# Level products of two heads in one group, in place, with the samples behind the last level and branch b first: a hybrid HGRN2 / RG-LRU layer

## The chip, the cores and the metric

One core of one Trainium2 chip. The metric is the device time of one execution in microseconds; a kernel's time is the median of its runs. The comparison is between the kernel before and the kernel after one change, both computing the same outputs.

## The reference

One layer of a decoder trunk runs on 512 prompt tokens and 8 sample tokens (one new token each for eight running sequences), all in fp32. Width is 1024, with eight heads of 128 and eight blocks of 128.

```python
h = _rmsnorm(x, norm1_g[l]) * (1.0 + sc1) + sh1
u = h @ w_in[l]                                  # 1024 x 8192
qa, fa, ia, oga, xb, yb, ga, gb = _split_cols(u)
# HGRN2: S_t = diag(f_t) S_{t-1} + k_t outer v_t,  o_t = S_t^T q_t
o, S_new = _hgrn2(q, k, v, logf, S0)
o_a = _rmsnorm(o, hg_onorm_g[l]) * silu(oga)
# RG-LRU: causal convolution, block-diagonal gates, then a linear recurrence
hseq, h_last = _rglru(xc, r, ig, lru_lambda[l], st_lru)
o_b = hseq * gelu(yb)
merged = sigmoid(ga) * (o_a @ w_branch_a[l]) + sigmoid(gb) * (o_b @ w_branch_b[l])
x = x + g1 * (merged @ w_out[l])
h2 = _rmsnorm(x, norm2_g[l]) * (1.0 + sc2) + sh2
x = x + g2 * (square(relu(h2 @ w_ff1[l])) @ w_ff2[l])
y = _rmsnorm(x, final_norm_g)
```

sh, sc and g come from a product of the conditioning vectors with w_mod (the modulation). The outputs are y for prompt and samples and the new states: the HGRN2 matrices, the RG-LRU vectors and the convolution's last inputs.

## The kernel before

Everything is kept with channels on the partitions and the 520 tokens (T = 512 + 8) in the free dimension. A big product is one 128 x 128 weight tile against 260 tokens (half of T). fp32 accuracy is had from three products of split operands: `whi` is the rounded weight (cast on ACT, L111), `wlo` the remainder (a subtraction on DVE, L114); activations are split in the same way (`split`, L200 on ACT and L201 on DVE). The helper `gemm` issues these products at L150.

The stages follow one another in one list of steps: the norm and modulation; then for h = 0 to 7 the head's four column blocks (f, q, g, v) and, in between, the blocks of RG-LRU (`rg_x`, `rg_y`); then eight merge gates (`ga`, part 6 of w_in), within which `end_recurrences` and `begin_tail` close the pools of the heads; then branch a (o_a times w_branch_a), the eight gates of part 7, and branch b; then w_out and the MLP. The order on each engine is set by a scheduler that puts work with a higher priority first (`urgent()` is an offset of 200) and otherwise follows the program. Weights are fetched ahead on SP's queue. `mod_step` puts parts of the second modulation's products (L408, on the `wst` buffers) between the steps of the tail.

A head's prompt part (`head_prompt`) works with blocks that double, from b = 1 to b = 64. At each level TensorE computes, for every block of 2b tokens, the attention between its two halves (K of the first half, Q of the second, L642 for b = 2 to 16, L656 for b = 1, L674 for b = 32 and L680 for b = 64). Then DVE multiplies one half of the Q and K rows by a running decay (L682), which writes the buffer Y from X, or X from Y at the next level; the half that isn't multiplied is copied along (L688; at b = 1 by ACT). `copy_predicated` (L690) puts the level's products into `a32` under a mask. After the last level the diagonal blocks go to `at`, K is transposed, the chunk states S are built, the outputs are made (L726 and L728), squared on ACT with a sum (L733), normalized by a small chain on DVE (L734 and L206 to L215, inverse square root) and scaled on ACT (L738), transposed (L742), and multiplied into the output gate (L744), which is stored to `oaT_d` in DRAM (L745).

The sample part of a head: v of the samples is transposed and copied (`vs`, L592), sent to DRAM and broadcast back to all partitions (`vd` L594, `vb` L596, both on SP's queue), and the state tiles `st` are scaled on ACT (L603) and updated on DVE (L604, eight per head); then 8 products (L610) give the outputs, which are copied to `sev`, transposed (L615) and put into `os` (L617).

In the tail, `load_branches` loads o_a and o_b back from DRAM on POOL's queue through five buffers `t` (L878 for o_a), and splits them into the tiles `a` (o_a) and `b` (o_b).

Of the kernel before, what the change touches and what calls it, by code (L numbers as in the profile page):

```python
# [28 lines left out]
URGENT = 200  # L29
NWM = 8  # L30
# [12 lines left out]
BUFS = {"e": 6, "g": 6, "xb": 1, "xc": 2, "xcs": 2, "gate": 4, "ag": 2, "hs": 3, "y": 3, "ma": 8, "rs": 1, "sq": 1, "t": 5, "sqs": 2,  # L43
# [32 lines left out]
class Kernel:  # L76
# [108 lines left out]
    def urgent(self):  # L185

        return self.tc.high_priority(offset=URGENT)

# [354 lines left out]

# [7 lines left out]
    def head(self, h, first=None):  # L551
# [17 lines left out]
        v = self.slot(self.hg, "e")  # L569
# [10 lines left out]
        fkq = self.fkq[h % 2]  # L580
# [3 lines left out]
        self.head_prompt(h, f, X, q, v, og)  # L584
        self.head_sample(h, st, vb, fkq)
# [14 lines left out]
    def head_sample(self, h, st, vb, fkq):  # L600
        nc = self.nc
        for b in range(NB):
            nc.scalar.activation(st[:, b], st[:, b], AF.Copy, scale=fkq[:, 0, b:b + 1])  # L603
            nc.vector.scalar_tensor_tensor(st[:, b], vb[:, b], fkq[:, 1, b:b + 1], st[:, b], OP.mult, OP.add)  # L604
        nc.sync.dma_start(self.o["hgrn_s"][0, :, h].rearrange("b k v -> k b v"), st)

        po = self.pps.tile([128, 512], F32, name="ps")
        for b in range(NB):
            j, c = 32 * (b % 4), 128 * (b // 4)
            nc.tensor.matmul(po[j:j + 32, c:c + 128], fkq[:, 2], st[:, b], start=True, stop=True)  # L610
        ev = self.hg.tile([128, 256], F32, name="sev")
        nc.scalar.copy(ev, po[:, :256])
        pt = self.ppt.tile([128, 512], F32, name="pt")
        for c in (0, 128):
            nc.tensor.transpose(pt[:, c:c + 128], ev[:, c:c + 128], self.ident)  # L615
        own = bass.AP(tensor=pt.tensor, offset=pt.offset, ap=[pt.ap[0], [132, 2], [33, 4]])
        nc.vector.tensor_copy(self.os[:, h].rearrange("p (a b) -> p a b", a=2), own)  # L617

    def head_prompt(self, h, f, X, q, v, og):
        nc = self.nc  # L620

        pv = self.pps.tile([128, 512], F32, name="ps")
        for c in range(NC):
            nc.tensor.transpose(pv[:, c * C:(c + 1) * C], v[:, c * C:(c + 1) * C], self.ident)
        vn = self.slot(self.hg, "g")
        nc.scalar.copy(vn[:, :L], pv)

        Y = self.hg.tile([128, 2, T], F32, name="Y", bufs=2)  # L630
        nc.vector.tensor_tensor(X[:, 0, :L], q[:, :L], f[:, :L], OP.mult)
        T_ = self.hg.tile([128, 508], F32, name="tb", bufs=2)
        tb, to = f[:, :L], 0
        a32 = self.hg.tile([128, NC, 32], F32, name="a32")
        at = self.at[h % 2]

        def block_level(x, y):
            p = self.pps.tile([128, 512], F32, name="ps")
            for c in range(NC):
                for j in range(4):  # L640
                    s = slice(c * C + 32 * j, c * C + 32 * j + 32)
                    nc.tensor.matmul(p[32 * j:32 * j + 32, c * 32:c * 32 + 32], x[:, s], y[:, s], start=True, stop=True)  # L642
            return p[:, :128].rearrange("p (c t) -> p c t", c=NC)
# [6 lines left out]

        p = self.pps.tile([128, 512], F32, name="ps")
        for c in range(NC):
            for j in range(4):
                s = c * C + 32 * j
                o = p[32 * j:32 * j + 32, c * 64:c * 64 + 64].rearrange("p (x t) -> p x t", x=2)
                nc.tensor.matmul(o, X[:, 1, s:s + 32], X[:, 0::2, s:s + 32], start=True, stop=True)  # L656
        first = p[:, :256].rearrange("p (c x t) -> p c x t", c=NC, x=2)
        nc.vector.tensor_tensor(a32, first[:, :, 1], self.mdiag, OP.mult)
        b = 1
        while b < C:  # L660
            Q, K = X[:, 0], X[:, 1]

            n = L // (2 * b)
            fac = bass.AP(tensor=tb.tensor, offset=tb.offset, ap=[tb.ap[0], [1, 2], [2, n], [0, b]])
            if b == 1:
                p = first[:, :, 0]
            elif b <= 16:
                p = block_level(K, Q)
            elif b == 32:
                p = self.pps.tile([128, 512], F32, name="ps")  # L670
                for c in range(NC):
                    for j in (0, 64):
                        s = c * C + j
                        nc.tensor.matmul(p[j:j + 32, c * 32:c * 32 + 32], K[:, s:s + 32], Q[:, s + 32:s + 64],  # L674
                                         start=True, stop=True)
            else:
                p = self.pps.tile([128, 512], F32, name="ps")
                for c in range(NC):
                    s = c * C
                    nc.tensor.matmul(p[:64, c * 64:c * 64 + 64], K[:, s:s + 64], Q[:, s + 64:s + 128],  # L680
                                     start=True, stop=True)
            nc.vector.tensor_tensor(view(Y, b, 0, 2 * b, n, b), view(X, b, 0, 2 * b, n, b), fac, OP.mult)  # L682
            if b == 1:
                nc.scalar.copy(view(Y, 0, 1, 2, n, 1), view(X, 0, 1, 2, n, 1))
            else:

                h2 = b // 2
                nc.vector.tensor_copy(view(Y, h2, b, 2 * b, n, h2), view(X, h2, b, 2 * b, n, h2))  # L688
            if b <= 16:
                nc.vector.copy_predicated(a32, self.masks[b], p)  # L690
            elif b == 32:
                for j in (0, 64):
                    nc.scalar.copy(at[j:j + 32, :, j + 32:j + 64],
                                   p[j:j + 32, :128].rearrange("p (c t) -> p c t", c=NC))
            else:
                nc.scalar.copy(at[:64, :, 64:], p[:64, :256].rearrange("p (c t) -> p c t", c=NC))
            t2 = tb.rearrange("p (n two) -> p n two", two=2)
            tn = T_[:, to:to + n]
            nc.vector.tensor_tensor(tn, t2[:, :, 0], t2[:, :, 1], OP.mult)
            tb, to = tn, to + n  # L700
            X, Y = Y, X
            b *= 2
        Q, K = X[:, 0], X[:, 1]
        for j in range(0, 128, 32):
            nc.vector.tensor_copy(at[j:j + 32, :, j:j + 32], a32[j:j + 32])
# [54 lines left out]
    def blockdiag_w(self, n):  # L760
        nc = self.nc
        r = []
        for name in ("lru_wa", "lru_wx"):
            st = self.hg.tile([128, 128], F32, name="bdst")
            nc.sync.dma_start(st, self.i[name][0, n])
            hi = self.hg.tile([128, 128], F32R, name="bdh" + name)
            lo = self.hg.tile([128, 128], F32R, name="bdl" + name)
# [7 lines left out]
    def blockdiag(self, w, x, bias):  # L775
        nc = self.nc
        o = self.slot(self.hg, "gate")
# [9 lines left out]
    def rg_x(self, n):  # L787
# [4 lines left out]
        xb = self.slot(self.hg, "xb")  # L792
        with self.urgent():
            nc.scalar.copy(self.two(xb), ps)
        xc = self.slot(self.hg, "xc")
# [9 lines left out]
        xs = self.split(xc, self.hg, "xcs")  # L805
# [5 lines left out]
    def rg_scans(self, ns):  # L811
# [3 lines left out]
        for n in ns:  # L815
            r = self.rg[n][0]
            a = self.slot(self.hg, "ag")
            self.grouped(nc.scalar.activation(a, r, AF.Exp, scale=self.c8n[:, n:n + 1]))
            self.grouped(nc.scalar.activation(r, r, AF.Tanh, scale=self.c8[:, n:n + 1]))
            u = self.slot(self.hg, "xc")  # L820
# [8 lines left out]
        for n, (a, u) in zip(ns, aa):  # L829
            g = self.rg[n][1]  # L830
            nc.vector.tensor_tensor(g, g, u, OP.mult)
            hs = self.slot(self.hg, "hs")
# [7 lines left out]
    def rg_y(self, n):  # L840
# [3 lines left out]
        t, y = self.slot(self.hg, "y"), self.slot(self.hg, "y")  # L844
# [29 lines left out]
    def load_branches(self):  # L874
        nc = self.nc
        for h in range(H):
# [3 lines left out]
            self.oa.append(self.split(t, self.ab, "a"))  # L880
        for n in range(KO):
            t = self.slot(self.tail, "t")
            nc.gpsimd.dma_start(t, self.obT_d[n])
            self.ob.append(self.split(t, self.abb, "b"))
# [11 lines left out]
    def merge(self, m, s, t1):  # L896
        self.branch("w_branch_b", m, self.ob, s)
# [652 lines left out]
    def run(self):  # L1550
# [39 lines left out]
        for m in range(KO):  # L1590
            one("w_in", 48 + m, lambda m: ga.update({m: self.gate(6, m, self.slot(self.ma, "ma"))}), m)
# [5 lines left out]
        for m in range(KO):  # L1597
            if m == 2:
                steps.append(([], self.rg_out))
            one("w_branch_a", m, lambda m: self.branch("w_branch_a", m, self.oa, ga[m]), m)  # L1600
            if m <= TAIL or m % 2:
                mod_step()
        for m in range(KO):
            one("w_in", 56 + m, lambda m: gb.update({m: self.gate(7, m, self.slot(self.tail, "t"))}), m)
            one("w_branch_b", m, lambda m: self.merge(m, gb.pop(m), ga.pop(m)), m)
# [24 lines left out]
    def begin(self):  # L1630
# [167 lines left out]
        self.hg = self.open_pool("hg", 2, reuse_waits="tile")  # L1798
        self.at = []
        self.fkq = [self.hg.tile([128, 3, 32], F32, name=f"fkq{n}", bufs=1) for n in range(2)]  # L1800
        for t in self.fkq:
# [70 lines left out]
```

## Time and profile before

| | |
|---|---|
| median of three runs | 1030.33 us (1029.38 to 1030.82) |
| profiled execution, its own time | 1028.26 us |
| its span | 1026.5 us |
| granted TensorE clock, mean | 0.997 |
| PE / DVE / ACT / POOL busy | 1004.4 / 691.1 / 520.4 / 123.3 us |
| heads, 62 to 420 us: PE busy | 356.71 of 358 us |

The profiled execution is one run of the program; its span is the time from its first to its last instruction. Busy times are of that span. L numbers are lines of the kernel; PE is TensorE's matmul, DVE VectorE, ACT ScalarE, POOL GpSimd, SP the queue from which most DMAs are issued. The records of small products come in twos: 16 matmuls of L642 are 32 records.

### The profile page before, as it was taken

How to read it: one execution, taken by the hardware profiler on the slowest of the kernel's cores; microseconds unless marked ns; L12 is line 12 of the kernel's file. 1: busy time of each engine (PE TensorE's matmuls, PEld its weight loads, DVE VectorE, ACT ScalarE, POOL GpSimd, SP SyncE). 2: the span in 40 equal slices, each digit the busy share in tenths (PEclk: the TensorE clock that was granted, in tenths of full speed). 3: DMA queues.
4: the chain of work that ended last, by engine and by line, in shares of the span. 5: the costliest groups of instructions: out<-in, count | busy, mean ns of one | idle time of the engine just before them, and what ended most of it. 6: DMA issues, size and time to landing. Idle time of an engine off the chain costs nothing. (4 is left out here: it accounts for less than half of the span.)

```text
span 1026.5 us, 23725 instructions
## 1 busy us (share of the span) xinstructions
PE 1004.4 (98%) x9756; PEld 967.8 (94%) x9756; DVE 691.1 (67%) x1520; ACT 520.4 (51%) x988; POOL 123.3 (12%) x228
## 2 busy tenths in 40 slices
PE   5999999999999999999999999999999999999997
PEld 3899999999999999988999999999999999999996
DVE  6788779596877868365233347677776776777685
ACT  4555743663575356342122235466556655656663
POOL 3200000000000000031000001011421231232150
PEclk9999999999999999999999999999999999999998
DMA  9673443434334324398555568222672484274242
GB/s 323 223 202 111 120 128 115 118 113 141 107 115 127 115 85 136 97 331 248 164 165 165 165 186 242 86 83 63 134 186 72 94 183 115 53 162 96 63 82 84
DMA packets 201823, 143.68 MB, mean 140 GB/s; under 512 B 6767, under 2 KB 189703, under 8 KB 201707
## 3 DMA queue, kind: packets, MB, share of 16 engines
q1 hardware_dynamic: 191090, 128.08, 41.7%
q0 software_dynamic: 10608, 14.05, 6.9%
q8 instruction: 76, 1.25, 0.5%
q14 instruction: 33, 0.26, 0.1%
q10 hardware_dynamic: 16, 0.03, 0.0%
HBM read 123.61 MB, written 11.26 MB: 131 GB/s over the span
## 5 line engine op out<-in xcount | busy, mean ns | idle before, releaser
L150 PE MATMUL mm<-h,whi 128*128 128x260 f32 (+1 forms) x2944 | 489.9, 285 | 0.0
L150 PEld LDWEIGHTS mm<-h,whi 128*128 128x128 f32 x2944 | 409.4, 188 | 4.8 <-ACT whi L111 3.3
L150 PE MATMUL mm<-h,wlo 128*128 128x260 f32 x1472 | 304.8, 286 | 0.3 <-DVE wlo L114 0.3
L111 ACT CAST whi<-wst 128x1024 fp32r<-128x1024 f32 x164 | 171.7, 1049 | 221.8 <-PE mm L150 172.9
L114 DVE TENSOR_TENSOR wlo<-wst,whi 128x1024 fp32r<-128x1024 f32 x164 | 200.0, 1220 | 108.7 <-ACT whi L111 107.6
L150 PEld LDWEIGHTS mm<-h,wlo 128*128 128x128 f32 x1472 | 230.2, 189 | 2.1 <-issue 0.8
L150 PE MATMUL mm<-a,whi 128*128 128x260 f32 x512 | 84.2, 285 | 0.0
L150 PEld LDWEIGHTS mm<-a,whi 128*128 128x128 f32 x512 | 70.3, 188 | 2.1 <-issue 1.2
L150 PE MATMUL mm<-a,wlo 128*128 128x260 f32 x256 | 51.9, 283 | 0.0
L878 POOL DMA_DIRECT2D t<-oaT_d x8 | 4.4, 552 | 384.1 <-ACT sq L751 376.4
L1271 DVE TENSOR_TENSOR f<-f 128x260 f32<-128x260 f32 x64 | 27.3, 427 | 27.6 <-ACT f L1266 26.9
L1260 ACT ACTIVATE ft<-ft,fsh 128x512 f32<-128x512 f32 (+2 forms) x36 | 24.0, 676 | 36.1 <-DVE ft L1257 36.1
L150 PE MATMUL mm<-b,whi 128*128 128x260 f32 x256 | 41.1, 282 | 0.0
L1263 POOL TENSOR_TENSOR ft<-ft,fsh 128x8 f32<-128x8 f32 x28 | 18.4, 658 | 188.2 <-DVE ft L1257 188.2
L150 PEld LDWEIGHTS mm<-a,wlo 128*128 128x128 f32 x256 | 39.5, 188 | 0.0
L150 PEld LDWEIGHTS mm<-b,whi 128*128 128x128 f32 x256 | 35.0, 188 | 0.0
L1305 POOL DMA_DIRECT2D ma<-snap x28 | 26.7, 968 | 38.3 <-issue 29.1
L1287 POOL DMA_DIRECT2D ma<-snap x28 | 25.9, 925 | 36.0 <-DMA ma<-snap 24.4
L603 ACT ACTIVATE st<-st,fkq 128x128 f32<-128x128 f32 x64 | 20.2, 390 | 16.6 <-DVE fkq L582 14.4
L1266 ACT ACTIVATE f<-ft 128x520 f32<-128x520 f32 (+1 forms) x36 | 20.8, 587 | 15.0 <-POOL ft L1264 13.0
L894 DVE TENSOR_TENSOR t<-mm,t 128x520 f32<-128x520 f32 x8 | 5.6, 700 | 30.5 <-PE mm L150 30.5
L150 PE MATMUL mm<-b,wlo 128*128 128x260 f32 x128 | 25.9, 284 | 0.0
(579 smaller groups left out, 1933.1 us busy)
## 6 DMA issues: line engine op xcount, KB each, us to landing
wst<-in_w_in_dram SPq DMA_DIRECT2D x64, 512.0 KB
wst<-in_w_mod_dram SPq DMA_DIRECT2D x32, 512.0 KB
wst<-in_w_ff_dram SPq DMA_DIRECT2D x64, 256.0 KB
wst<-in_w_ff_dram SPq DMA_DIRECT2D x32, 512.0 KB
wm<-in_w_mod_dram SPq DMA_DIRECT2D x16, 512.0 KB
st<-in_state_hgrn_dram SPq DMA_DIRECT2D x8, 512.0 KB
vb<-vd SPq DMA_DIRECT2D x8, 512.0 KB
out_dram<-st SPq DMA_DIRECT2D x8, 512.0 KB
```

Source lines behind the costliest of these rows:

```text
L111: ins = self.nc.scalar.copy(hi, st)
L114: self.nc.vector.tensor_tensor(lo, st, hi.bitcast(F32), OP.subtract)
L150: self.last_product = self.nc.tensor.matmul(ps[s][:, :c.stop - c.start], x, y[:, c], start=first and n == 0, stop=last and n == 2)
L603: nc.scalar.activation(st[:, b], st[:, b], AF.Copy, scale=fkq[:, 0, b:b + 1])
L878: nc.gpsimd.dma_start(t[:, :L], self.oaT_d[h])
L894: self.nc.vector.tensor_tensor(self.two(s), ps, self.two(s), OP.mult)
L1260: nc.scalar.activation(t[:, :p], t[:, :p], AF.Relu, bias=sh[:, 0:1])
L1263: eng.tensor_tensor(t[:, p:], t[:, p:], sh[:, 1:9], OP.add)
L1266: nc.scalar.activation(f, self.two(self.ft)[:, a:a + n], AF.Square)
L1271: self.nc.vector.tensor_tensor(f[:, n], f[:, a], f[:, b], op)
L1287: nc.gpsimd.dma_start(x[1][:, b], v[:, :n], accum_op=OP.add)
L1305: nc.gpsimd.dma_start(x[t][:, a], s[p], accum_op=OP.add)
```

## The change

In the heads: the prompt part is called once for two heads, (h - 1, h), after the second head's inputs are there. At each level the products of both heads form one group (`together()`, priority offset 400): 32 products for b = 1 to 16, 16 for b = 32, 8 for b = 64, and behind the last the samples' 16 products of both heads (L623). Q and K are multiplied in place: Y, the copies of L688 and the ACT copy at b = 1 are gone, and X has four buffers. `a32` and `at` hold both heads, and one `copy_predicated` serves two heads. f and v move to `ma` buffers, the RG-LRU's tiles to a pool of their own, and the samples' transposes (L632) come after both heads' outputs. The samples' state update (L597) is issued before the levels.

In the tail: the eight gates issued in the heads' pools are now part 7, and branch b comes first; the merge then adds branch a. o_b is loaded into the tiles `a`, o_a into `b`.

```diff
-BUFS = {"e": 6, "g": 6, ...
+BUFS = {"e": 4, "g": 6, ...
+    def together(self):
+        return self.tc.high_priority(offset=TOGETHER)
...
-        f = self.slot(self.hg, "e")
-        X = self.hg.tile([128, 3, T], F32, name="X", bufs=2)
+        f = self.slot(self.ma, "ma")
+        X = self.hg.tile([128, 3, T], F32, name="X", bufs=4)
...
-        self.head_prompt(h, f, X, q, v, og)
-        self.head_sample(h, st, vb, fkq)
+        ... (transposes of v, vn, X[:, 0] = q * f)
+        for b in range(NB):
+            nc.scalar.activation(st[:, b], st[:, b], AF.Copy, scale=fkq[:, 0, b:b + 1])
+            nc.vector.scalar_tensor_tensor(st[:, b], vb[:, b], fkq[:, 1, b:b + 1], st[:, b], OP.mult, OP.add)
+        nc.sync.dma_start(self.o["hgrn_s"][0, :, h].rearrange("b k v -> k b v"), st)
+        self.opened[h] = f, X, vn, og, st, fkq
+        if h % 2:
+            self.heads_prompt((h - 1, h))
...
+        while b < C:
+            p = self.pps.tile([128, 512], F32, name="ps")
+            with self.together():
+                for e, X in enumerate(Xs):
+                    ... (all products of the level for head e)
+                if b == 64:
+                    po = self.heads_sample(hs)
+            for X, tb in zip(Xs, tbs):
+                half = view(X, b, 0, 2 * b, n, b)
+                nc.vector.tensor_tensor(half, half, fac, OP.mult)
...
-            nc.vector.tensor_tensor(view(Y, b, 0, 2 * b, n, b), view(X, b, 0, 2 * b, n, b), fac, OP.mult)
-            if b == 1:
-                nc.scalar.copy(view(Y, 0, 1, 2, n, 1), view(X, 0, 1, 2, n, 1))
-            else:
-                h2 = b // 2
-                nc.vector.tensor_copy(view(Y, h2, b, 2 * b, n, h2), view(X, h2, b, 2 * b, n, h2))
...
+        for e, h in enumerate(hs):
+            self.head_prompt(h, tbs[e], at[:, e])
+        self.heads_sample_done(hs, po)
...
-            self.oa.append(self.split(t, self.ab, "a"))
+            self.ob.append(self.split(t, self.ab, "a"))    # o_b loaded first, o_a behind it into "b"
...
-            one("w_in", 48 + m, ... self.gate(6, m, ...ma
+            one("w_in", 56 + m, ... self.gate(7, m, ...ma
-            one("w_branch_a", m, lambda m: self.branch("w_branch_a", m, self.oa, ga[m]), m)
+            one("w_branch_b", m, lambda m: self.branch("w_branch_b", m, self.ob, gb[m]), m)
...
-        self.at = []
-        self.fkq = [... for n in range(2)]
+        self.fkq = [... for n in range(4)]
+        self.at = self.hg.tile([128, 2, NC, C], F32, name="at", bufs=1)
```

The lines move with it: L150 before is L151 after, L642 and L674 are L669, L656 is L664, L680 (the products of b = 64) is L673, L610 is L623, L615 is L632, L682 is L680, L690 is L687, L592 is L608, L604 is L597, L728 is L732, L742 is L746, L744 is L748 and L408 is L413.

TensorE in the middle of the heads, before: head 0's output transposes (L742) and the first levels of head 1, in two groups of 16 products.

```order
L656 MATMUL ps<-X 32x64 x6
L742 MATMUL pt<-ident,g 128x128 x4
L656 MATMUL ps<-X 32x64 x10
L150 MATMUL mm<-h,whi 128x260
L150 MATMUL mm<-h,wlo 128x260 x2
L150 MATMUL mm<-h,whi 128x260 x4
L150 MATMUL mm<-h,wlo 128x260 x2
L150 MATMUL mm<-h,whi 128x260 x4
L150 MATMUL mm<-h,wlo 128x260
L642 MATMUL ps<-Y 32x32 x6
L615 MATMUL pt<-ident,sev 128x128 x2
L642 MATMUL ps<-Y 32x32 x10
```

TensorE, after, first and second level of a middle pair, heads 4 and 5 (L787 is a block-diagonal product of the RG-LRU):

```order
L664 MATMUL ps<-X 32x64 x32
L787 MATMUL pb<-xcs,bdhlru_wx 128x260 x2
L787 MATMUL pb<-xcs,bdllru_wx 128x260
L151 MATMUL mm<-h,wlo 128x260
L151 MATMUL mm<-h,whi 128x260 x4
L151 MATMUL mm<-h,wlo 128x260 x2
L151 MATMUL mm<-h,whi 128x260 x4
L151 MATMUL mm<-h,wlo 128x260 x2
L151 MATMUL mm<-h,whi 128x260 x3
L669 MATMUL ps<-X 32x32 x32
```

The groups hold twice the products, and nothing stands inside them any more.

DVE, before, in the last head: the copy of vs, the first levels and the samples' updates (L604).

```order
L592 COPY vs<-ps 8x128
L744 TENSOR_TENSOR e<-pt,e 128x512
L808 TENSOR_TENSOR gate<-gate,xc 128x520
L834 TENSOR_TENSOR hs<-ag,pa 128x8
L617 COPY os<-pt 128x8
L658 TENSOR_TENSOR a_5570<-ps,mdiag 128x128
L682 TENSOR_TENSOR X<-Y,tb 128x2x128x2
L690 COPY_PREDICATED a_5570<-mask_185,ps 128x128
L604 SCALAR_TENSOR_TENSOR st<-vb,fkq_739,st 128x128 x6
L688 COPY X<-Y 128x2x128
```

DVE, after, in the pair of heads 4 and 5 (L680 is now the level's multiplication, of X in place; L597 the samples' update):

```order
L608 COPY vs<-ps 8x128
L680 TENSOR_TENSOR X<-X,ma 128x2x256 x2
L597 SCALAR_TENSOR_TENSOR st<-vb,fkq_742,st 128x128 x8
L683 TENSOR_TENSOR a_3966<-ps,mdiag 128x256
L773 TENSOR_TENSOR bdllru_wx<-bdst,bdhlru_wx 128x128
L812 TENSOR_TENSOR gate<-gate,xc 128x520
L838 TENSOR_TENSOR hs<-ag,pa 128x8
L680 TENSOR_TENSOR X<-X,tb 128x2x128x2
L687 COPY_PREDICATED a_3966<-mask_185,ps 128x256
L115 TENSOR_TENSOR wlo<-wst,whi 128x1024
L680 TENSOR_TENSOR X<-X,tb 128x2x128x2
```

All eight updates of the second head of a pair now stand between its first and its second level, as one run.

TensorE, before, at the end of the last head:

```order
L742 MATMUL pt<-ident,g 128x128 x4
L150 MATMUL mm<-h,whi 128x260
L150 MATMUL mm<-h,wlo 128x260 x2
L150 MATMUL mm<-h,whi 128x260 x4
L150 MATMUL mm<-h,wlo 128x260 x2
L150 MATMUL mm<-h,whi 128x260 x4
L150 MATMUL mm<-h,wlo 128x260 x2
L150 MATMUL mm<-h,whi 128x260 x4
L150 MATMUL mm<-h,wlo 128x260 x2
L150 MATMUL mm<-h,whi 128x260 x4
L150 MATMUL mm<-h,wlo 128x260 x2
L615 MATMUL pt<-ident,sev 128x128 x2
```

TensorE, after, at the same place (L413 are modulation products; `mm<-a` is the first product of the first branch):

```order
L151 MATMUL mm<-h,whi 128x260 x4
L151 MATMUL mm<-h,wlo 128x260 x2
L746 MATMUL pt<-ident,g 128x128 x4
L632 MATMUL pt<-ident,sev 128x128 x4
L413 MATMUL pt<-wst,cT 32x256 x15
L757 MATMUL ps<-sq_5988,ones_r 128x64
L413 MATMUL pt<-wst,cT 32x256
L870 MATMUL ps<-ident,xlast 11x128 x2
L151 MATMUL mm<-a,whi 128x260 x4
```

The 27 big products between L742 and the samples' transposes are gone from there, and behind the transposes the first branch follows with modulation products and two transposes between. From L728 of the last head to L742 there are 74 big products before; from L732 to L746 there are 28 after.

More of the change, by code (lines that the diff above doesn't have):

```diff
@@ L598, in head_sample_v, with heads_sample @@
         return vb
-    def head_sample(self, h, st, vb, fkq):
+    def heads_sample(self, hs):
         nc = self.nc
[L602 to L605, printed above, removed]
         po = self.pps.tile([128, 512], F32, name="ps")
[L608 to L612, printed above, removed]
+        for e, h in enumerate(hs):
+            *_, st, fkq = self.opened[h]
+            for b in range(NB):
+                j, c = 32 * (b % 4), 256 * e + 128 * (b // 4)
+                nc.tensor.matmul(po[j:j + 32, c:c + 128], fkq[:, 2], st[:, b], start=True, stop=True)
+        return po
@@ L619, in head_prompt, with heads_prompt @@
-    def head_prompt(self, h, f, X, q, v, og):
+        own = bass.AP(tensor=pt.tensor, offset=pt.offset, ap=[pt.ap[0], [256, 2], [132, 2], [33, 4]])
+        nc.vector.tensor_copy(self.os[:, hs[0]:hs[0] + 2].rearrange("p e (a b) -> p e a b", a=2), own)
+    def heads_prompt(self, hs):
         nc = self.nc
[L622 to L643, printed above, removed]
@@ L648, in view @@
                            ap=[t.ap[0], [T + first_k - first_q, 2], [step, n], [1, b]])
[L651 to L657, printed above, removed]
@@ L875, in load_branches @@
         nc = self.nc
+        for n in range(KO):
+            t = self.slot(self.tail, "t")
+            nc.gpsimd.dma_start(t, self.obT_d[n])
+            self.ob.append(self.split(t, self.ab, "a"))
         for h in range(H):
```

143 lines of the change are left out of this document (81 added, 62 removed).

## The prediction

> **What bounds the kernel now.** I read the page first, then the table of stretches for the head phase, then TensorE's timeline around single groups of small products, then its waits, and last the timelines of the place where the heads end. The page:
>
> ```profile
> span 1026.5 us, 23725 instructions
> PE 1004.4 (98%) x9756; PEld 967.8 (94%) x9756; DVE 691.1 (67%) x1520; ACT 520.4 (51%) x988; POOL 123.3 (12%) x228
> PEclk9999999999999999999999999999999999999998
> ```
>
> TensorE is busy for 98% of the span at a clock that is full nearly throughout. The table of stretches (stretch, length, then busy time of PE, PEld, DVE, ACT and POOL, clock, DMA share, GB/s) has the eight heads in its first row here and the start of the tail in its second:
>
> ```profile
> 62.00:420.00 358.00, 356.71 (x4237) 342.46 (x4235) 271.53 (x745) 198.29 (x421) 0.00 (x0) 1.00 0.41 120
> 433.00:460.00 27.00, 27.00 (x240) 24.34 (x239) 15.06 (x38) 10.55 (x17) 9.63 (x17) 1.00 0.93 309
> ```
>
> In the heads PE idles for 358.00 - 356.71 = 1.3 us; DVE for 86. So nothing that the change takes from DVE or ACT can shorten the heads by more than 1.3 us; it must shorten PE's own stream. And each wait that it puts in front of PE counts in full.
>
> **Part 1: fewer groups of small products.** What a group costs is seen between big products. PE's timeline (start, length, instruction):
>
> ```profile
> 66.97 0.53 PE L150 MATMUL mm<-h,whi 128*128 128x260 f32 x3
> 67.43 0.65 PE L656 MATMUL ps<-X 128*32 128x64 f32 x32
> 67.90 0.48 PE L642 MATMUL ps<-Y 128*32 128x32 f32 x32
> 68.31 0.39 PE L150 MATMUL mm<-h,whi 128*128 128x260 f32 x1
> 68.53 0.40 PE L150 MATMUL mm<-h,wlo 128*128 128x260 f32 x2
> ...
> 75.01 0.41 PE L150 MATMUL mm<-h,wlo 128*128 128x260 f32 x2
> 75.25 0.64 PE L150 MATMUL mm<-h,whi 128*128 128x260 f32 x4
> 75.82 0.46 PE L642 MATMUL ps<-X 128*32 128x32 f32 x32
> 76.20 0.51 PE L150 MATMUL mm<-h,wlo 128*128 128x260 f32 x2
> 76.55 0.64 PE L150 MATMUL mm<-h,whi 128*128 128x260 f32 x4
> ```
>
> Two big products take 75.25 - 75.01 = 0.24 us, so 0.12 each. From 75.25 to 76.55 lie six of them (0.72) and one group of L642 (32 records of 16 products): 1.30 - 0.72 = 0.58 us for the group. The records follow one another closely: the group's bar is 0.46 long and one record 0.199 (next row), so 31 steps fill 0.26 and one step is 8.4 ns; 32 of them are 0.27.
>
> ```profile
> L642 PE MATMUL ps<-X 128*32 128x32 f32 x512 | 7.5, 199 | 0.0
> ```
>
> What is left, 0.58 - 0.27 = 0.31 us, is paid for entering and leaving the run of small products, whatever stands in it. The two adjacent groups check it: 66.97 to 68.53 is 1.56 us with four big products (0.48), so 1.08 for L656 and L642 together; L642 alone would be 0.58, and L656's 32 records of twice the columns then add 0.50, which is near 2 x 8.4 ns x 32 = 0.54 with no second entry. The order has 62 such runs before (eight groups in each head; in two places two of them touch) and 29 after (seven in each pair, and one extra). 33 fewer x 0.31 = **-10.2 us**. In the two middle pairs the 64-row products of level 64 and the 32-row products of the samples alternate once more (4, 1, 4, 7 products): two more changes of shape at about 0.1 each, **+0.2**. If these changes within a run cost a full 0.31, it is +0.6.
>
> The Trainium skill, page "TensorEngine Tiling (Array Packing)", section "Key Properties", says that "changing tiling mode (not just tile) drains the TensorE". This agrees with the 0.31 us; it would speak against the alternation, since each change there is one of mode, and by it the +0.2 would be +0.6 and the whole sum 0.4 higher.
>
> **Part 2: copies and temporaries on DVE.** In place, the 48 copies go, 14.6 us, and the level multiplications stay:
>
> ```profile
> L688 DVE COPY X<-Y 128x256 f32<-128x256 f32 x24 | 7.7, 322 | 0.0
> L688 DVE COPY Y<-X 128x256 f32<-128x256 f32 x24 | 6.9, 287 | 0.0
> L682 DVE TENSOR_TENSOR Y<-X,tb 128x512 f32<-128x512 f32 x24 | 16.4, 682 | 0.1
> L604 DVE SCALAR_TENSOR_TENSOR st<-vb,fkq,st 128x128 f32<-128x128 f32 x64 | 18.6, 344 | 8.9 <-DMA vb<-vd 8.9
> L114 DVE TENSOR_TENSOR wlo<-wst,whi 128x1024 fp32r<-128x1024 f32 x164 | 200.0, 1220 | 108.7 <-ACT whi L111 107.6
> ```
>
> That DVE had 86 us of idle time there, so this is worth 0 by itself (one wait aside). PE's waits have one row in the head phase that goes, because the samples' transposes (L615, L632 after) no longer stand right behind L742 in the early heads: **-1.0 us**.
>
> ```profile
> PE pt L615 <- DVE e L744: 1.0, 1, 1.0
> ```
>
> **Part 3: the level chain in place.** Before, L682 wrote the other buffer, so DVE could run a level ahead of PE. Now L680 may overwrite X only when PE has read it, and PE's next level needs that result: PE group, two L680, PE group, in turn. In the order of after, 35 big products (4.2 us) and a group of 32 products (about 0.9) lie between levels: 5.1 us. DVE has to fit two L680 (1.4), one weight half (1.22, about one in 44 products), a mask copy and some small products into it. That fits, with little left, except where DVE itself stands. It stands at the samples' eight L597, moved ahead of the second level, which need vb, broadcast through DRAM. Before, they did so too but with X already a level ahead:
>
> ```profile
> 334.95 0.28 DVE L592 COPY vs<-ps 8x128 f32<-8x128 f32 x1
> 335.26 0.30 SPq L594 DMA_DIRECT2D vd<-vs  x1
> 337.43 0.35 SPq L596 DMA_DIRECT2D vb<-vd  x1
> 341.45 0.61 DVE L604 SCALAR_TENSOR_TENSOR st<-vb,fkq,st 128x128 f32<-128x128 f32 x2 [2.06 <-DMA vb<-vd]
> ```
>
> vb can be used 341.45 - 335.23 = 6.2 us after vs was copied, of which DVE then idled 2.06. In the middle pairs (heads 2,3 and 4,5) after has, on PE, the products of vs, 20 big products (2.4), the first level's group (to about 4.1 us, counted from the start of the products of vs), 19 big products, the next group, 35 big products, and then the level b=4, whose second head is wanted at 11.9. DVE: vs copied at 0.6; vb at 6.6 (0.6 + about 6.0); eight L597 at 18.6 / 64 = 0.29 each, to 8.9; the mask product, a block-diagonal half, gate and scan pieces, about 1; L680 of the first head to 10.6; the weight half 1.22 and L680 of the second head to 12.7. So PE stands about 0.9 us in each of two pairs: **+1.8 us**. The bounds: 0 where vb comes a microsecond sooner, and 5 where every later level of the pair starts late as well (four pairs by 1.2). Pairs 0 and 3 have 28 to 43 products of room, so I take only the two.
>
> **Part 4: where heads end and the tail begins.** The sample transposes of a pair now stand behind both heads, and less work is left behind them: between the last head's output products (L732) and L746 lie only 28 big products (74 before), and straight behind L746 come L632, sixteen modulation products, and then the first branch, which needs the tail's pools. The timelines of before:
>
> ```profile
> 420.89 0.39 PE L728 MATMUL pt<-g,Y 128*128 128x128 f32 x2
> 421.32 0.28 ACT L733 ACTIVATE g<-pt 128x128 f32<-128x128 f32 x1 [3.24 <-PE pt L728]
> 422.49 0.17 DVE L734 TENSOR_SCALAR ss<-ss 128x4 f32<-128x4 f32 x1 [3.66 <-ACT g L733]
> 424.48 0.16 DVE L214 TENSOR_TENSOR rs_t<-rs_t,rs_h 128x4 f32<-128x4 f32 x1
> 424.79 0.60 ACT L174 ACTIVATE ma<-mm 128x520 f32<-128x520 f32 x1
> 426.31 1.14 ACT L738 ACTIVATE g<-pt,rs_y 128x128 f32<-128x128 f32 x4 [0.92 <-DVE rs_y L215]
> 430.04 0.60 PE L742 MATMUL pt<-ident,g 128*128 128x128 f32 x4
> 430.40 0.37 PE L150 MATMUL mm<-h,whi 128*128 128x260 f32 x1
> 430.68 0.69 DVE L744 TENSOR_TENSOR e<-pt,e 128x512 f32<-128x512 f32 x1 [4.46 <-PE pt L742]
> 434.13 0.17 DVE L617 COPY os<-pt 128x8 f32<-128x8 f32 x1 [1.63 <-PE pt L615]
> 444.04 0.55 POOL L878 DMA_DIRECT2D t<-oaT_d  x1 [5.07 <-DVE t L879]
> 449.64 0.63 ACT L200 CAST a<-t 128x520 fp32r<-128x520 f32 x1 [2.02 <-DMA t<-oaT_d]
> 449.81 1.07 PE L408 MATMUL pt<-wst,cT 128*32 128x256 f32 x16
> 450.81 0.75 PE L150 MATMUL mm<-a,whi 128*128 128x260 f32 x4
> ```
>
> (a) L746 waits for the norm: squares, a chain on DVE, L742 on ACT. From 420.89 the chain could end its last step at 424.84 (L214 plus one more of its kind), then a gate (0.5 of it left) and 1.14 on ACT: 426.4. 28 products end at 424.5: **1.9**. (b) L632 uses the one PSUM tile that L748 must empty; L742 to the end of L744 took 431.37 - 430.04 = 1.33, of which PE's four products fill 0.36: **1.0**. (c) The first L413 waits for the copy of that tile: four products 0.60 and 0.17, less the overlap: **0.5**. (d) Call the end of L748 T. The first cast of branch b may write only when the last head's store of its output is done (pool memory shared with the gate buffers). No row shows that store; the nearest are vd (2.2 us from issue to the next step, 335.26 to 337.43) and the 256 KB load (5.6, 444.04 to 449.64). I take 2.2, as nothing else moves at this time: cast 0.63, half 0.69 (like L744), hand-offs 0.4: first product at T + 3.9, where sixteen modulation products (1.9, twice the 1.00 of eight; the 16 records of 449.81 are eight products) end at T + 3.5: **0.4**; at 5.6 it would be 3.0 more. (e) Five t buffers: the sixth load is issued when the first half is made, T + 4.0, and takes 5.6 as above, since all eight loads run at once; with the cast it is there at T + 10.2, where PE, at six products for each tile (0.72), wants it at T + 7.8: **2.4**; 0 if the load takes 2.2 as vd did. Together **+6.2 us**, bounds 3.4 and 9.5.
>
> The Trainium skill, page "DMA: Bandwidth & Descriptors", section "Anatomy of one DMA — SWDGE (gpsimd) path", gives about 2.0 us plus bytes / 436e3; for 256 KB that is an estimate of 2.6 us, under half the 5.6 seen here beside a DMA share of 0.93. By the page, term (e) would be 0 and the sum -5.4.
>
> **Sum.** -10.2 + 0.2 - 1.0 + 1.8 + 6.2 = **-3.0 us**. All terms at their low ends give -7.6, at their high ends +3.5. The profiled execution took 1028.26 us (span 1026.5) and would become 1025.3; the runs shown have a median of 1030.33, 2.1 above it, so I forecast **1027.3**, with a range of its own of 1022.7 to 1033.8.
>
> **Rivals.** *A: both new waits are hidden.* vb arrives sooner in a freer queue, and the scheduler's order leaves the tail's loads early enough. For it: PE waits for almost nothing in the heads today. Against: term (a) has no cover in the order. -10.2 + 0.2 - 1.0 = -11.0: 1019.3 us. *B: slower, because the chain in place is bound by DVE.* At each of 24 steps (four pairs, six levels after the first) PE waits for DVE. DVE was busy 271.5 of 358 us, about 0.71 of it without the copies: 3.6 of the 5.1 us between levels; and it waited for ACT's cast 108.7 / 164 = 0.66 us at each weight half, which makes 4.3. From 0.8 us more in a step PE stands. If each step were late by 0.5, it is 24 x 0.5 = +12: -11.0 + 6.2 + 12 = +7: 1037.5 us. For it: in-order DVE, no second buffer. Against: 1.4 us of slack a step on average. *C: the change doesn't do what it says: the price goes with the products, not with the run.* Then the 33 runs fewer save nothing, and parts 3 and 4 stand: 0.2 - 1.0 + 1.8 + 6.2 = +7.2: 1037.5 us. Against it: the 1.08 us of the two adjacent groups.
>
> **How the numbers follow.** Forecast 0.50, A 0.15, B 0.22, C 0.13. A measurement of this kernel can tell about 0.2% (2.1 us) from no change. The forecast's spread puts 0.31 of its 0.50 below that line, 0.13 inside and 0.06 above. A is all faster. B's and C's 0.35 are slower but for 0.05 (a milder B, a part of C). Faster 0.46, same 0.18, slower 0.36. The range goes from 1020.0 (A's upper part) to 1037.0 (most of B and C): it leaves out some 2 in 10.
>
> **What would show it.** In the profile after: 29 runs of small products, each of 32 records of 32 columns at about 0.58 plus 0.27 us; if a pair's group costs twice a single head's, C. PE's waits on L680: two of 0.9 is the forecast, twenty of 0.5 is B. PE's waits at L746, L632, L413 and the first product of branch b: 1.9, 1.0, 0.5 and 2.8. The forecast is wrong as a whole if PE waits somewhere that none of these parts names, or if the first branch waits for the store by 5 us or more.

## The result and the profile after

The change makes no difference that can be told: 1030.84 us (median of 12 runs, 1027.48 to 1033.11) against 1030.28 for the kernel before (12 runs, 1028.41 to 1032.80), ratio 1.0005, 95% interval 0.9992 to 1.0018. The forecast was 1027.3 with a range of 1020 to 1037.

The page of the changed kernel, and its table of stretches for the heads and for three pieces behind them:

```profile
span 1027.4 us, 23569 instructions
PE 997.1 (97%) x9756; PEld 965.4 (94%) x9756; DVE 677.3 (66%) x1428; ACT 514.0 (50%) x964; POOL 123.8 (12%) x229
```

```profile
62.00:420.00 358.00, 354.49 (x4292) 346.91 (x4292) 257.13 (x645) 192.62 (x399) 4.23 (x7) 1.00 0.43 126
440.00:444.00 4.00, 1.49 (x11) 1.04 (x11) 1.25 (x5) 1.64 (x5) 0.00 (x0) 1.00 0.00 0
444.50:448.00 3.50, 3.42 (x30) 1.44 (x30) 1.20 (x3) 2.09 (x5) 0.18 (x1) 0.54 0.48 159
452.00:456.00 4.00, 1.98 (x16) 1.23 (x15) 1.14 (x6) 0.98 (x2) 0.00 (x0) 1.00 0.97 345
```

TensorE has 7.3 us less to do (1004.4 before, 997.1 now), and the span is 0.9 longer: what was saved came back as time in which it stands. In four microseconds from 440 it is busy for 1.49, and just behind, its granted clock is 0.54. TensorE's waits say for what it stood:

```profile
PE ps L669 <- DVE X L680: 3.4, 5, 0.9
PE mm L151 <- ACT a L205: 2.0, 1, 2.0
PE pt L746 <- ACT g L742: 1.7, 1, 1.7
PE pt L632 <- DVE e L748: 0.8, 1, 0.8
PE pt L413 <- DVE os L634: 0.3, 1, 0.3
```

None of these was there before; the one row of before in the heads (L615, 1.0) is gone.

What a group costs now, in TensorE's timeline of the second pair:

```profile
211.92 0.52 PE L151 MATMUL mm<-h,whi 128*128 128x260 f32 x3
212.37 0.76 PE L669 MATMUL ps<-X 128*32 128x32 f32 x64
213.06 0.39 PE L151 MATMUL mm<-h,whi 128*128 128x260 f32 x1
213.29 0.40 PE L151 MATMUL mm<-h,wlo 128*128 128x260 f32 x2
```

From 211.92 to 213.29 are 1.37 us; four big products take 0.48, so 64 records cost 0.89, where two groups of 32 cost 2 x 0.58 = 1.16. So the pair's group saves 0.27, where 0.31 had been estimated.

The end of the heads, in TensorE's timeline (the last column is the idle time ahead and what ended it):

```profile
442.21 0.66 PE L746 MATMUL pt<-ident,g 128*128 128x128 f32 x4 [1.73 <-ACT g L742]
443.65 0.66 PE L632 MATMUL pt<-ident,sev 128*128 128x128 f32 x4 [0.78 <-DVE e L748]
444.57 3.50 PE L413 MATMUL pt<-wst,cT 128*32 128x256 f32 x30 [0.27 <-DVE os L634]
...
452.89 0.62 PE L413 MATMUL pt<-wst,cT 128*32 128x256 f32 x2
455.53 0.51 PE L151 MATMUL mm<-a,whi 128*128 128x260 f32 x2 [2.02 <-ACT a L205]
455.97 0.63 PE L413 MATMUL pt<-wst,cT 128*32 128x256 f32 x6
...
457.44 0.64 PE L413 MATMUL pt<-wst,cT 128*32 128x256 f32 x8
```

Three waits come within 4.4 microseconds, 2.8 us in all, and then thirty records of modulation products take 3.5 us, while sixteen took 1.07 before. The next sixteen records are cut into 2, 6 and 8.

The middle pairs, on DVE: the samples' updates start when vb is there, and the second level's multiplications come with a weight half between them.

```profile
196.73 2.19 DVE L597 SCALAR_TENSOR_TENSOR st<-vb,fkq,st 128x128 f32<-128x128 f32 x8 [1.77 <-DMA vb<-vd]
...
200.06 0.68 DVE L680 TENSOR_TENSOR X<-X,tb 128x512 f32<-128x512 f32 x1
200.67 0.44 DVE L687 COPY_PREDICATED a<-mask,ps 128x256 f32<-128x256 uint8 x1
201.00 1.21 DVE L115 TENSOR_TENSOR wlo<-wst,whi 128x1024 fp32r<-128x1024 f32 x1
202.13 0.68 DVE L680 TENSOR_TENSOR X<-X,tb 128x512 f32<-128x512 f32 x1
```

TensorE waited for the last of these for 0.86 us; it is the longest of the five waits on L680.

### The profile page after: what moved, and what is told of

Same layout as the page of the kernel before. It is cut to its first block, busy times and chain, and to the rows that moved or that the text cites. A ratio compares the mean times of both kernels' runs of the same rounds, so it can differ in the third digit from the quotient of the medians.

```text
span 1027.4 us, 23569 instructions
## 1 busy us (share of the span) xinstructions
PE 997.1 (97%) x9756; PEld 965.4 (94%) x9756; DVE 677.3 (66%) x1428; ACT 514.0 (50%) x964; POOL 123.8 (12%) x229
## 5 line engine op out<-in xcount | busy, mean ns | idle before, releaser
L151 PE MATMUL mm<-h,whi 128*128 128x260 f32 (+1 forms) x2944 | 489.5, 285 | 0.1
L151 PEld LDWEIGHTS mm<-h,whi 128*128 128x128 f32 x2944 | 409.1, 188 | 4.5 <-ACT whi L112 3.3
L151 PE MATMUL mm<-h,wlo 128*128 128x260 f32 x1472 | 301.9, 284 | 0.0
L112 ACT CAST whi<-wst 128x1024 fp32r<-128x1024 f32 x164 | 171.9, 1049 | 206.7 <-PE mm L151 178.8
L151 PEld LDWEIGHTS mm<-h,wlo 128*128 128x128 f32 x1472 | 230.1, 189 | 0.6 <-issue 0.4
L151 PE MATMUL mm<-a,whi 128*128 128x260 f32 x512 | 84.3, 285 | 2.0 <-ACT a L205 2.0
L151 PEld LDWEIGHTS mm<-a,whi 128*128 128x128 f32 x512 | 70.4, 188 | 4.6 <-ACT a L205 2.5
L151 PE MATMUL mm<-a,wlo 128*128 128x260 f32 x256 | 52.3, 284 | 0.0
L882 POOL DMA_DIRECT2D t<-obT_d x8 | 4.4, 550 | 384.5 <-PE ps L623 343.1
L151 PE MATMUL mm<-b,whi 128*128 128x260 f32 x256 | 41.1, 282 | 0.0
L151 PEld LDWEIGHTS mm<-a,wlo 128*128 128x128 f32 x256 | 39.6, 188 | 0.0
L151 PEld LDWEIGHTS mm<-b,whi 128*128 128x128 f32 x256 | 35.0, 188 | 0.0
L680 DVE TENSOR_TENSOR X<-X,tb 128x512 f32<-128x512 f32 x48 | 31.7, 681 | 0.0
L597 DVE SCALAR_TENSOR_TENSOR st<-vb,fkq,st 128x128 f32<-128x128 f32 x64 | 17.5, 345 | 13.5 <-DMA vb<-vd 13.5
```

The lines of the kernel that those rows point to most:

```text
L112: ins = self.nc.scalar.copy(hi, st)
L151: self.last_product = self.nc.tensor.matmul(ps[s][:, :c.stop - c.start], x, y[:, c], start=first and n == 0, stop=last and n == 2)
L680: nc.vector.tensor_tensor(half, half, fac, OP.mult)
```

## The experiments

Each is compared with the kernel before on the same chip. The experiments ran on three chips, so a distance from the changed kernel is taken between ratios: the experiment's less 1.0005, times 1030 us. The waits and timelines are those of one profiled execution of each kernel.

**Is the price one of the run?** One more product between the halves of twenty groups, held behind the first head's products and ahead of the second's:

```diff
+                    if e and 1 < b <= 32:
+                        between = nc.tensor.matmul(p[:, 384:], self.ident, X[:, 0, :128], start=True, stop=True)
...
```

> The changed kernel with one more 128 x 128 product (into unused columns, 0.11 us) put between the two heads' halves of each of the 20 groups from b = 2 to b = 32: each group is two runs of small products again. Theory (price by the run, 0.29 us): +20 x (0.11 + 0.29) = +8 us in the groups, each 1.29 instead of 0.89. Rival C (price goes with the products): +20 x 0.11 = +2.2.

1033.60 us, ratio 1.0036 (1.0024 to 1.0048), +3.2 us against the changed kernel. TensorE's timeline of one group:

```profile
112.56 0.28 PE L151 MATMUL mm<-h,wlo 128*128 128x260 f32 x1
112.77 0.46 PE L675 MATMUL ps<-X 128*32 128x32 f32 x32
113.16 0.49 PE L661 MATMUL ps<-X,ident 128*128 128x128 f32 x2
113.58 0.46 PE L675 MATMUL ps<-X 128*32 128x32 f32 x32
113.97 0.39 PE L151 MATMUL mm<-h,wlo 128*128 128x260 f32 x1
```

From the group's start to the next big product it is 1.20 us (112.77 to 113.97), against 0.69 in the changed kernel (212.37 to 213.06): +0.51. The extra product is two records, 0.22 at the step of 0.11 that such records have in a row, so 0.29 is for the second run: the theory's figure, and rival C, which has +0.22, is out. In twenty groups that is +10 us, more than the expected 8 since the product has two records, and yet the kernel lost only 3.2: its scheduler had put other work around, TensorE's waits on the level multiplications fell to 1.7 us, the one at the output transposes to 0.3, the wait of 2.0 on branch b's sixth tile (L205) was gone, and the clock stayed at 1.00 behind the heads. That was the first sign that several microseconds lie in the waits alone.

**The order of branches.** The tail's order of before under the new levels, and the reverse:

> The new levels with the tail's order of before: gates of part 6 and branch a first. Theory: the waits at L746, L632 and L413 stay (1.7, 0.8, 0.3), since they come from the heads; the first branch now needs the last head's output itself, stored (2.6 us) and loaded again (2.5 to 5.6 us): PE waits there 3 to 6 us instead of 2.0, and the time is 2 to 4 us above the changed kernel, 1033.5. Rival (the order of branches does not matter, the loads are late in both): the same, 1031.

> The kernel before with only the tail's order changed: gates of part 7 and branch b first, o_b in a, o_a in b. Theory (the waits at the end of the heads come from the pairs, not from the order of the branches): 74, 27 and 22 big products still cover L742, L615 and the modulation, and 92 more stand ahead of the first branch; no wait over 1 us there: 1029.5, within 1 us of before. Rival (branch b first is what costs): 3 us or more of waits at L150 mm<-a, 1034.

With the old tail: 1037.08 us, ratio 1.0076 (1.0056 to 1.0097), about 7 us above the changed kernel and more than expected; its four runs spread from 1034.3 to 1041.6. The waits at L746 and L632 stay at 1.7 and 0.8; the modulation ahead of the first branch now waits for its weights, the branch itself for only 0.8 us; a wait of 1.2 us on a mask copy (L687) came in the levels as well:

```profile
PE pt L413 <- DMA wst<-in_w_mod_dram: 5.2, 4, 2.6
```

With old levels and the new tail: 1030.32, ratio 1.0013 (0.9999 to 1.0026), and TensorE waits there for nothing but L615 (1.0 us, as before). So branch b first costs nothing by itself, and is worth about 7 us once the pairs have left the end of the heads uncovered; the waits come from the pairs.

**Modulation products as cover**, that is, as work for TensorE while the last head's chain runs on the other engines. Their rows gather in another PSUM bank, which lets the scheduler move them ahead:

```diff
-            self.psm = self.ppt.tile([128, 512], F32, name="pt")
+            self.psm = self.ppb.tile([128, 512], F32, name="pb")
```

> The changed kernel, but the modulation rows of the tail gather in the PSUM bank pb instead of pt, so they need not wait for the last head's transposes; the order then has 38 big and 12 modulation products between L732 and L746 instead of 28 and none. Theory (the gain is given back at the end of the heads): PE's waits at L746, L632 and L413 (1.7, 0.8, 0.3 us in the changed kernel) go to under 0.5 in all, the granted clock stays at 1.00 there (0.54 in the changed kernel between 444.5 and 448), and 16 records of modulation take about 1.1 us again. But the tiles of branch b come no sooner, so the wait on L205 grows from 2.0 to about 5; net about -1.5 us: 1029.3. Rival (the slow modulation products come from their own tiles or weights, not from PE's idle time before them): 30 records still take 3.5 us.

1028.73 us, ratio 1.0004 (0.9990 to 1.0017): nothing gained that can be told. The scheduler moved so many of them ahead that the sixth weight tile had not come; the clock then fell again (the waits, and a later stretch):

```profile
PE pb L413 <- DMA wst<-in_w_mod_dram: 2.9, 2, 2.7
```

```profile
452.00:456.00 4.00, 3.44 (x20) 1.69 (x18) 2.12 (x8) 0.26 (x1) 0.00 (x0) 0.50 1.02 357
```

This profile is of the slowest of the nine runs, 1032.71 us; five of them took 1027.8 to 1028.7, and whether they stood and slowed down in the same places is not shown. The rival, that modulation products are slow by themselves, is out: 24 records took 1.50 us in this kernel ahead of its idle time.

**Staging the last three tiles of branch b**, alone and with the edit above:

```diff
-            t = self.slot(self.tail, "t")
+            t = self.slot(self.tail, "t") if n < 5 else self.slot(self.abb, "b")
```

> The changed kernel, but the last three tiles of branch b are loaded into free b buffers, so their loads are issued with the first five and do not wait for a t buffer. Theory: the 2.0 us wait on L205 goes, and the modulation products behind it are less cut up; -2 to -3 us: 1028.3. Rival (the loads are late because the DMA engines are full there, share 1.02): the wait stays, or moves to the weights.

> Both of the two edits before. Theory: no wait over 1 us is left at the end of the heads except one for the store of the last head's output (about 1 us, since PE gets there sooner), the clock stays full: 4.8 us of waits, 1.6 of slow clock and about 1 of cut modulation groups go, about 1 comes: -6 us, 1024.8. Rival: the chain of the last head (L746, L748, store, cast) sets the time by itself and PE only waits elsewhere: no more than -2.

Alone: 1031.95, ratio 1.0017 (1.0008 to 1.0026). The wait of 2.0 became waits of 0.3, 0.2 and 0.5 on casts and halves of later tiles, and the modulation was cut into more pieces. Together: 1031.03, ratio 1.0008 (0.9996 to 1.0019), with the 2.7 us wait on modulation weights and one of 2.0 on DVE. Both theories' numbers were missed.

**Big products as cover.** The last two of the gates of part 7 (m = 6 and 7) are held back, product by product, behind the last head's K-V products (`kv`), its output products (`out`) and its output transposes (`turned`):

```diff
+                if self.hold:
+                    self.held += 1
+                    for skip, ins in self.hold:
+                        if self.held > skip:
+                            self.behind(self.last_product, ins)
...
+        self.hold, self.held = {6: [(24, kv), (40, out)], 7: [(0, out), (39, turned)]}.get(m if part == 7 else 0, ()), 0
```

Nothing is added or taken away; 21, 16, 47 and 9 big products then stand in the last head's four gaps (30, 35, 28 and 0 in the changed kernel).

> The changed kernel with the loads of the second edit (last three tiles of branch b staged in free b buffers) and with big products of the last two gates held back until late in the last head: 47 big products between L740 (the L732 of the changed kernel) and the output transposes (28 in the changed kernel), 9 between these and the samples' transposes (none). The modulation rows stay behind them in pt. Theory (PE has no cover there, and its idle time also costs it the clock): the waits of 1.7, 0.8 and 0.3 go, the clock stays at 1.00, the 2.0 at the sixth tile goes as in the second edit, and at most 1 us for the store of the last head's output comes: 4.8 + 1.6 - 1 = -5 to -7 us, about 1024.5. Rival (the first two edits failed since the tail itself is bound by DMA there, weights and tiles together): a wait for branch b's tiles or weights of 3 us or more takes their place, and the time stays near 1030.

> The held-back gates of e5_cover_stage alone, without staging branch b's last tiles. Theory (the five t buffers make the sixth load late, whatever stands ahead): PE gets to the first branch sooner, and the sixth tile, loaded some 9 us after the first half is made, makes it wait 3 us or more; of e5's 4.9 us at most 3 remain, 1028. Rival (the staging did nothing, as e2 alone suggests): 1026.

With staging: 1025.87 us, ratio 0.9959 (0.9944 to 0.9974), -4.7 us against the changed kernel. Without: 1023.64, ratio 0.9949 (0.9935 to 0.9963), -5.8 in four runs, faster than both kernels; the two intervals overlap, so what staging adds or costs here is not shown. The expectation that the sixth tile would make TensorE wait was wrong: behind the products held back, its loads came in time. The end of the heads without staging, in TensorE's timeline, and the stretch there:

```profile
438.89 0.66 PE L754 MATMUL pt<-ident,g 128*128 128x128 f32 x4 [0.26 <-ACT g L750]
440.45 0.60 PE L639 MATMUL pt<-ident,sev 128*128 128x128 f32 x4
441.31 1.93 PE L420 MATMUL pt<-wst,cT 128*32 128x256 f32 x32 [0.27 <-DVE os L641]
447.97 0.74 PE L153 MATMUL mm<-a,whi 128*128 128x260 f32 x4 [0.39 <-ACT whi L112]
```

```profile
440.00:444.00 4.00, 3.73 (x49) 2.52 (x48) 0.93 (x3) 2.00 (x5) 0.00 (x0) 1.00 0.32 107
```

Waits of 0.26, 0.27 and 0.39 are left of 1.73, 0.78, 0.27 and 2.02: -3.9 us. 32 modulation records take 1.93 us at clock 1.00, where 30 took 3.50 at 0.54: -1.7 (30 of them would be 1.8). Together that is 5.6 of the 6.6 us between the two profiled spans (1027.4 and 1020.8); the modulation groups are also cut up less.

**The waits in the middle pairs.** The second head's updates behind level b = 2:

> The changed kernel with the second head's eight sample updates (L597) put behind the multiplications of level b = 2 on DVE instead of ahead of them. Theory (DVE stands at vb in the two middle pairs): the two waits of about 1.0 us at level b = 4 of the middle pairs go, the three others (two of 0.7 in the first pair, 0.6 in the last) stay: -2 us, 1028.9. Rival B (the chain in place is bound by DVE as a whole): the same wait comes at a later level, 0.

1031.09 us, ratio 1.0012 (1.0003 to 1.0021). The waits on L680 (L693 here) fell by 1.4, and TensorE's wait at the output transposes grew by 2.4, since the new order left 6 big products there in place of 28:

```profile
PE pt L761 <- ACT g L757: 4.1, 1, 4.1
PE ps L682 <- DVE X L693: 2.0, 4, 0.7
```

The cause of the middle waits is supported, but not all of it: at the same level 0.65 and 0.51 us stay (0.86 and 0.80 in the changed kernel), now behind fewer big products. And the time as a whole did not fall, since the wait at the end of the heads grew by more.

**The change of shape inside a run.**

> The changed kernel with the samples' products (128*32) behind all of level 64's (128*64) in each group, so that the middle pairs change shape once, not three times. Theory (a change of shape within a run costs about 0.24 us): the two middle groups fall from 2.75 to 2.28, -0.9 us in all. Rival (the 0.47 is a wait for the samples' states): they stay at 2.75, 0.

1030.49 us, ratio 1.0005 (0.9996 to 1.0013): inconclusive as it stands, because the scheduler split level 64's group in both middle pairs. But the experiment before gives what was wanted. There, by chance, the second pair has its 64-row products in one piece and the third pair in two (4, 1, 4 and 15 products; the 7 of the prediction should have been 15), and in the changed kernel the second pair is in two:

```profile
223.14 1.15 PE L686 MATMUL ps<-X 128*64 128x64 f32 x16
224.22 1.08 PE L622 MATMUL ps<-st,fkq 128*32 128x128 f32 x32
225.23 0.75 PE L151 MATMUL mm<-h,whi 128*128 128x260 f32 x4
```

```profile
223.45 0.68 PE L673 MATMUL ps<-X 128*64 128x64 f32 x8
224.06 0.41 PE L623 MATMUL ps<-st,fkq 128*32 128x128 f32 x2
224.39 0.68 PE L673 MATMUL ps<-X 128*64 128x64 f32 x8
225.00 1.07 PE L623 MATMUL ps<-st,fkq 128*32 128x128 f32 x30
```

From the last big product ahead to the second behind, less 0.12 each, the first takes 2.28 us and the second 2.75: two more changes of shape, 0.47, so 0.24 for one. The changed kernel says the same by itself: its first and last pairs, with these products in one piece, take 2.28 too.

The trace of this run shows one thing more. Its end of the heads is that of the changed kernel, with the same three waits, but the clock fell elsewhere: the thirty modulation records behind the waits ran at 1.00, and the stretch at half the clock came 11 us later, behind the wait of 2.0 us on the sixth tile (the waits, and that stretch):

```profile
442.19 0.66 PE L747 MATMUL pt<-ident,g 128*128 128x128 f32 x4 [1.72 <-ACT g L743]
443.63 0.66 PE L633 MATMUL pt<-ident,sev 128*128 128x128 f32 x4 [0.78 <-DVE e L749]
444.55 1.93 PE L413 MATMUL pt<-wst,cT 128*32 128x256 f32 x30 [0.27 <-DVE os L635]
456.00:459.30 3.30, 3.30 (x20) 2.26 (x19) 2.86 (x14) 0.64 (x2) 1.08 (x2) 0.50 1.07 382
```

So the same waits are not always followed by a slow stretch at once.

**All of it:** big products as cover, staging, late updates, samples behind level 64.

> e5_cover_stage with the sample updates behind level b = 2 (as in e6) and the samples' products behind level 64's (as in e7). Theory: the end of the heads stays as in e5, two waits of about 1 us in the middle pairs become 0.5 to 0.8, two extra changes of shape (0.47) go in each middle pair: -1.5 us against e5, 1024.4. Rival: each edit moves the scheduler's order and gives as much away elsewhere: 1026.

1024.02 us, ratio 0.9953 (0.9940 to 0.9965): no better than the cover alone. The time is near the theory's 1024.4, but by the ratios it is only 0.6 us below cover with staging, and the two intervals overlap, so neither theory nor rival is shown by the time. The trace has what the rival describes: waits on L680 are at 2.6 (3.3 there), and a wait of 1.6 for a cast of the weights (L112) stands at the first branch, as one of 1.0 did with cover and staging: the tiles loaded early push the weights back, it seems, which no run separates.

## Why the prediction was right, and where it was not

The forecast was -3.0 us and the result +0.5, within its range: the saving was found, and most of the waits that eat it were found where they were said to be. The sum was 3.5 us too low, for two terms that were mis-sized and two things that no term named. A faster kernel had been held the likeliest, at 0.46; no difference that can be told had 0.18, and it is the width of the range that takes it in.

- *33 runs fewer, -10.2, and two changes of shape each in the middle pairs, +0.2.* Added up over all groups of the levels and samples (each from the last big product ahead to the second behind, less 0.12 a product), they cost 42.7 us before (the transposes among them taken off at 0.11 a record) and 33.4 after without the waits: -9.3, where -10.0 was the sum. The alternation makes the difference: it is 2 x 0.47 = +0.9 instead of +0.2. The term was mis-sized twice: it took two changes of shape at 0.1 for both middle pairs together, where there are two in each, and a change measures 0.24. The rule of the Trainium skill, page "TensorEngine Tiling (Array Packing)", section "Key Properties", that a change of tiling mode drains TensorE, pointed to +0.6 in that count; the trace agrees with it better than with the price that I took.
- *L615's wait, -1.0.* Gone as forecast.
- *Waits on X, +1.8.* The two in the middle pairs are 0.86 and 0.80 us, at the place given; putting the updates later took off 0.2 to 0.3 of each, so the reason given holds at least for a part. But three more came, 0.63 and 0.67 in the first pair at b = 32 and 0.43 in the last: L680 stands in DVE's queue behind scans and weight halves of 1.2 us. I had given pairs 0 and 3 as safe by counting big products only. They are 3.4 in all, within the bound of 5. Rival B had twenty-four steps late; five were.
- *The end of the heads, +6.2.* (a) 1.7 for 1.9, (b) 0.8 for 1.0, (c) 0.3 for 0.5, (d) 0 for 0.4: TensorE was still busy with the modulation when the store had ended, 2.6 us behind L748 (2.2 forecast), and where the modulation ran at full clock (the run of the change of shape) it did not stand there either; (e) 2.0 for 2.4. Sum 4.8, inside its bounds.
- *What no term named.* First the clock: in the profiled execution TensorE stood for 2.8 of 4.4 us and was then granted 0.54 of its clock; 30 records took 3.5 instead of 1.8 us, +1.7. The Trainium skill, page "TensorE: Matmul & The Clock Gate", section "Part 1: The HAM clock gate", says that the clock halves after an idle window of about 3.4 us. Here no single wait was that long; in two other runs, too, a stretch at 0.50 came behind shorter ones, waits of 0.63 and 0.67 us (modulation products as cover, in the first pair) and of twice 1.17 us (old tail, in the second). So in these traces less idle time was enough. Which waits are followed by a slow stretch is not fixed: the run of the change of shape has the same end of the heads and differs in it, so 1.7 is one execution's figure. All runs together bear out its size: the granted clock is 0.9946 in the mean of the changed kernel's 12 runs and 0.9964 to 0.9969 in the means of the kernel before on three chips, and (1 - clock) times the span, an estimate of the time lost to it, is 5.6 us against 3.2 to 3.7.
- *Also named by no term:* the modulation products behind were cut into 2, 6 and 8 records among the first branch's, 2.3 us for what a group of 16 costs in one piece (1.2): +1.1. I had priced them by the group of before and not by the order of after, in which the cuts could be read.

Together: -9.3 - 1.0 + 3.4 + 4.8 + 1.7 + 1.1 = +0.7 us. The profiled spans differ by +0.9, of which 0.4 stand before the heads begin, where nothing was changed; the medians of 12 runs differ by +0.6, with an interval of -0.8 to +1.9. Rival A's 1019.3 needs the waits hidden: the cover alone took them down to 0.9 at the end of the heads and gave 1023.6.

## What to carry to other kernels

When a change shortens the busiest engine's own stream, ask which products will stand behind the last chain of the stage: here the same big products, only held back until that chain needed them, were worth about 6 us where the whole change was worth none. Price a wait on TensorE with what can follow it, since a few microseconds at half the clock came behind several of the waits here. And read from the order of the changed kernel not just what moved but what was cut up.

## What the runs showed of the hardware

- Entering and leaving a run of small products costs 0.27 to 0.31 us, in runs of 32 and of 64 records (0.58 and 0.89 us in all, and 0.29 for one more run of 32); a change of shape inside a run costs 0.24.
- After 2.8 us of waits within 4.4 us TensorE's granted clock was 0.54 over the next 3.5 us, and four modulation records took 0.43 us instead of 0.22. In another run the same waits were followed by a clock of 1.00, and a stretch at 0.50 came behind a later wait of 2.0 us. In the six profiles without such a stretch between 60 and 480 us (the kernel before, old levels, one more product, and the three with cover) no single wait there was longer than 1.6 us, but waits as short as 0.63 and 0.67 us, close together, were followed by one in another.
